# Mixture experts ranked by token count on the chip, with two slot groups for the three emptiest

## The chip, the cores and the metric

The kernel runs on one core of a Trainium2 chip. The metric is device microseconds (us) of one execution; the time given is the median of the timed runs, and one further execution was profiled. The core's engines are named as in the profile: PE (matrix multiply; PEld is its weight load), DVE (vector), ACT (activations), POOL, and SP, which here does little but issue DMAs. [...]

## The reference

A decoder trunk of two layers over 256 tokens of width 1024: retention, a dense SwiGLU, a gated short convolution, and then a mixture of 8 experts, of which each token takes 2. Cut to the mixture, this is what must come out:

```
def _swiglu(xn, w_gate, w_up, w_down):
    return (jax.nn.silu(xn @ w_gate) * (xn @ w_up)) @ w_down

def _moe_swiglu(xn, w_router, w_gate_e, w_up_e, w_down_e):
    logits = (t @ w_router).astype(jnp.float32)      # t: 256 x 1024, 8 experts
    top_vals, top_idx = lax.top_k(logits, TOP_K)     # TOP_K = 2
    gates = ...                                      # softmax over the two
    for e in range(N_EXPERTS):
        h = jax.nn.silu(t @ w_gate_e[e]) * (t @ w_up_e[e])
        out = out + gates[:, e:e + 1] * (h @ w_down_e[e])
```

Each expert has three matrices of 1024 x 3584 float32, 44 MB together. All weights are float32 and are read once. 512 token places (256 tokens, 2 experts each) fall on 8 experts; evaluated with its own inputs, the reference's router gives experts 0 to 7 the counts 60, 62, 69, 73, 65, 53, 76 and 54.

## The kernel before

All weights lie in DRAM as 426 pieces of 1 MiB (128 partitions x 2048 float32): 90 for the dense layers, then 336 for the mixture, 42 for each expert. SP streams them in the order in which they are used (`dma_next`, line 109) into a ring of 14 SBUF tiles called `raw`; three pieces of the mixture's first steps go into spare tiles called `xT` as well. A piece is issued when the tile that it needs has been freed by its last reader, so the ring is at most 14 pieces ahead of PE. SP takes its instructions strictly in order.

The mixture works on gathered tokens. `select` (line 617) marks each token's two experts on DVE, `positions` (line 633) gives each token its slot within its expert, `one_hot` and `gather` (line 673) collect the tokens of an expert into a tile `X` with 96 slots (CAP), three groups of 32. Expert 0 is gathered before the loop, the other seven inside it, in the `hooks` between pieces (`extras`, line 796).

The loop (line 829) has 56 steps, seven for each expert. A step takes four gate and up pieces (`moe_gate_up`) and then the two down pieces of the step before (`moe_down`). The slot groups are the stationary operand, 32 columns at a time, and four matmuls stand beside each other in the four column quarters of the array. So a gate and up piece costs 2 x 3 x 4 matmuls, of which four run at once, and the loop over the groups, `for g in range(NG)` and `for r in range(3)`, sets the count. An expert with 60 tokens takes as long as one with 76.

```
for k in range(2):
    kb = 2 * q + k
    for g in range(NG):
        for j in range(4):
            self.mm(o[g][32 * j:32 * j + 32], X[:, kb, 32 * g:32 * g + 32], w[:, k, j], ...)
```

When an expert is done, `scale_y` (line 717) splits its output on ACT and DVE; one quarter of it lies on partitions 96 to 127 and goes through `yraw` and three small DMAs on ACT's queue into `yq`. `scatter` (line 736) returns the rows to the tokens in two halves, in the next expert's steps 1 and 2. `posrow` and `onehT` hold the positions of one expert, spread over the partitions, for that. The last expert has a form of its own, `last_scatter`. A branch at the end (`fallback`) does the tokens beyond the 96th of any expert; no expert has that many here.

Of the kernel before, what the change touches and what calls it, by code (L numbers as in the profile page):

```python
# [8 lines left out]
F32 = mybir.dt.float32  # L9
# [7 lines left out]
P = 128  # L17
# [11 lines left out]
C_PART = 2640  # L29
C_ALL = 2644  # L30
# [11 lines left out]
NG = CAP // 32  # L42

# [11 lines left out]
class Trunk:  # L55
    def __init__(self, ctx, tc, w, x, gT, gfin, convw, router, cst, eoh, out):
        self.ctx, self.tc, self.nc = ctx, tc, tc.nc
        self.w, self.x, self.convw, self.gfin = w, x, convw, gfin
        self.router, self.cst, self.eoh, self.out, self.gT_dram = router, cst, eoh, out, gT
        self.order = consumption_order()  # L60
        pool = lambda name, bufs, **k: ctx.enter_context(tc.tile_pool(name=name, bufs=bufs, **k))
        self.rawp = pool("raw", R_BUFS)
        self.com = pool("common", 1)
        self.sm = pool("small", 4)
        self.dense = ExitStack()
        pool = lambda name, bufs, **k: self.dense.enter_context(tc.tile_pool(name=name, bufs=bufs, **k))
# [4 lines left out]
        self.raw, self.W = {}, {}  # L71
        self.extra = set()
        self.n_dma = self.n_split = 0
        self.la, self.limit = LA, 2 * N_DENSE - 1
# [524 lines left out]
    def moe(self, base, ev, mp):  # L599
# [8 lines left out]
        lg, sel, off, pos, gts = (small(n, [2, 8]) for n in ("lg", "sel", "off", "pos", "gts"))  # L608
        rs = []
        part = mp.tile([P, 1 + NG], F32, name="part")  # L610
# [6 lines left out]
        def select(tb):  # L617
            nc.vector.tensor_copy(lg[:, tb], pl[tb][:, 0:8])
            le = lg[:, tb, :, None].to_broadcast([P, 8, 8])
            lo = lg[:, tb, None, :].to_broadcast([P, 8, 8])  # L620
            c1 = mp.tile([P, 8, 8], F32, name="c1")
            c2 = mp.tile([P, 8, 8], F32, name="c2")
            rank = mp.tile([P, 8], F32, name="rank")
# [4 lines left out]
            nc.vector.tensor_reduce(rank, c1, axis=AX.X, op=OP.add)  # L628
            nc.vector.tensor_scalar(sel[:, tb], rank, 2.0, None, op0=OP.is_lt)
# [3 lines left out]
        def positions():  # L633
            self.mm(pp[:, 8:16], LT, sel[:, 1], False, True)
            nc.vector.tensor_scalar(off, sel, -1000.0, 1000.0, op0=OP.mult, op1=OP.add)
            nc.vector.tensor_tensor(pos, off, pp[:, 0:16].rearrange("p (a b) -> p a b", a=2), op=OP.add)

        def one_hot(pr, t):
            nc.vector.tensor_tensor(t, iota[:, None, None, :].to_broadcast([P, 2, 2, P]),
                                    pos[:, :, 2 * pr:2 * pr + 2, None].to_broadcast([P, 2, 2, P]), op=OP.is_equal)  # L640
# [14 lines left out]
        def gates2():  # L655
            nc.vector.tensor_tensor(ex, ex, sel, op=OP.mult)
            nc.vector.tensor_reduce(mx, ex, axis=AX.X, op=OP.add)
            nc.vector.reciprocal(mx, mx)
            nc.vector.tensor_tensor(gts, ex, mx[:, :, None].to_broadcast([P, 2, 8]), op=OP.mult)

# [3 lines left out]
        def overflow1():  # L664
            nc.vector.tensor_scalar(fl, pos, CAP - 0.5, None, op0=OP.is_gt)
            nc.vector.tensor_tensor(fl, fl, sel, op=OP.mult)
            nc.vector.tensor_reduce(fr, fl, axis=AX.XY, op=OP.add)
# [26 lines left out]
        def save_positions():  # L694

            self.posT = self.dram.tile([8, S], F32, name="posT")
            for tb in range(2):
                nc.scalar.dma_start(self.posT[:, tb * P:(tb + 1) * P].rearrange("e t -> t e"), pos[:, tb])
# [6 lines left out]
        def slots2(e):  # L705
            row = PT[e]
            if e == NE - 1:
                PT[e] = self.com.tile([P, NG, S], F32R, name="xT", bufs=3)
                for g in range(NG):
                    nc.vector.tensor_scalar(PT[e][:, g], row, part[:, 1 + g:2 + g], None, op0=OP.is_equal)  # L710
            else:
                PT[e] = mp.tile([P, S], F32R, name="onehT")
                nc.vector.tensor_scalar(PT[e], row, part[:, 0:1], None, op0=OP.is_equal)
# [3 lines left out]
        def scale_y(e, accs):  # L717


            yH, yL = (self.xp.tile([P, D], F32R, name=n) for n in ("yH", "yL"))  # L720
            raw = self.xp.tile([P, 768], F32, name="yraw")
# [8 lines left out]
            Y[e] = yH, yL  # L730
# [5 lines left out]
        def scatter(e, hf):  # L736
            f = slice(hf * 512, (hf + 1) * 512)
            ps = [self.ps() for _ in range(2)]
            for tb in range(2):
                for a in range(2):  # L740
                    self.mm(ps[tb], PT[e][0:CAP, tb * P:(tb + 1) * P], Y[e][a][0:CAP, f], a == 0, a == 1)
            for tb in range(2):
                nc.vector.scalar_tensor_tensor(self.h[:, tb, f], ps[tb], gts[:, tb, e:e + 1], self.h[:, tb, f],  # L743
                                               op0=OP.mult, op1=OP.add)

        def last_scatter(accs):
# [3 lines left out]
            for g in (0, 2, 1):  # L750
                self.split(yH[:, g], yL[:, g], accs[g // 2][:, g % 2 * 256:g % 2 * 256 + 256])
            gu = [self.gup.tile([P, 512], F32, name="gu") for _ in range(4)]
            outs = [gu, [self.bank(), self.bank(), self.ps(), self.ps()]]
            for tb in range(2):
                for g in (0, 2, 1):
# [23 lines left out]
        for hf in range(2):  # L779
# [5 lines left out]
                                pos[:, :, 0, None].to_broadcast([P, 2, CAP]), op=OP.is_equal)  # L785
        self.moe_pools()
        for kb in range(0, 8, 2):
            gather(0, (kb, kb + 1), (0,))
        nc.vector.tensor_tensor(t[:, :, 1, 0:CAP], iota[:, None, 0:CAP].to_broadcast([P, 2, CAP]),
                                pos[:, :, 1, None].to_broadcast([P, 2, CAP]), op=OP.is_equal)  # L790
        save_positions()
        nc.scalar.dma_start(part, self.cst[:, C_PART:C_ALL])

        late = {}

        def extras(s):
# [7 lines left out]
            if s == 0:  # L804
                f = {1: gates1}
# [25 lines left out]
        for s in range(MU * NE):  # L831
            e, u = divmod(s, MU)
            hooks = extras(s)
            if s == COUNT_AT:
                n_over = nc.values_load(self.ovf[0:1, 0:1], min_val=0, max_val=NE * S)
            o = self.moe_gate_up(at, XP[e // 2][:, :, e % 2], hooks)
            at += 4
            new = self.moe_swiglu(o)
            if hid is not None:
                if u == 1:  # L840
                    accs = [self.bank(), self.bank()]
                self.moe_down(at, hid, accs, (s - 1) % MU, (s - 1) // MU == NE - 1)
# [3 lines left out]
            hid = self.moe_hid_T(new)  # L846
        gfin = self.com.tile([P, D], F32, name="xT", bufs=3)
        nc.sync.dma_start(gfin, bass.AP(tensor=self.gfin.tensor, offset=self.gfin.offset, ap=[[0, P], [1, D]]))
        self.moe_down(at, hid, accs, MU - 1, True)
# [8 lines left out]
        for hf in range(2):  # L858
            for tb in range(2):
                for q in range(2 * hf, 2 * hf + 2):  # L860
                    hs = self.h[:, tb, q * 256:(q + 1) * 256]
                    nc.vector.scalar_tensor_tensor(hs, outs[tb][q][:, 0:256], gts[:, tb, NE - 1:NE], hs,
# [17 lines left out]
        self.fallback(n_over, mp, pos, gts, tH, tL, iota)  # L880
# [8 lines left out]
    def moe_gate_up(self, at, X, hooks):  # L889


        A, B = (self.gup.tile([P, 512], F32, name="gu") for _ in range(2))
        o = (A[:, 0:256], A[:, 256:512], B[:, 0:256])
        for q in range(4):
            w = self.raw[at + q].rearrange("p (k j c) -> p k j c", k=2, j=4)
            for k in range(2):
                kb = 2 * q + k
                for g in range(NG):
# [4 lines left out]
        return A.rearrange("p (g u c) -> p g u c", g=2, u=2), B[:, 0:256].rearrange("p (g u c) -> p g u c", g=1, u=2)  # L903
# [9 lines left out]
    def moe_hid_T(self, hid):  # L913

        T = self.xp.tile([P, NG, P], F32, name="hT", bufs=2)
        self.nc.vector.transpose(T.rearrange("p g c -> p (g c)"), hid.rearrange("p g c -> p (g c)"))  # L916
        return T

    def moe_down(self, at, T, accs, u, quarters):
# [3 lines left out]
        for d in range(2):  # L923
            w = self.raw[at + d].rearrange("p (k c) -> p k c", k=2)
            for k in range(2):
                j = 2 * d + k
                first, last = u == 0 and j == 0, u == MU - 1 and j == 3
                for r in range(3):
                    o = accs[r // 2][:, r % 2 * 256:r % 2 * 256 + 256]
                    for t in range(4):  # L930
                        g, c = (r, t) if quarters else (t, r) if t < 3 else (r, 3)
# [122 lines left out]
def constants():  # L1054
# [22 lines left out]
    p = np.arange(P)  # L1077
    c[:, C_PART] = p
    for g in range(NG):
# [87 lines left out]
```

## Time and profile before

| | us |
|---|---|
| median of 3 runs | 1483.62 (1483.21 to 1484.95) |
| the profiled execution's own time | 1484.88 |
| its span, first to last instruction | 1483.2 |
| PE busy in the span | 1463.4 (99%) |
| DVE, ACT busy | 461.9 (31%), 304.0 (20%) |

The span has three stretches: the dense layers up to about 540 us, the routing and the first gather up to 558.85 us, and the mixture's loop up to 1467.5 us, after which 15.7 us remain for the last scatter, the final norm and the output. The page's 40 slices are 37 us each. Its DMA row is the mean busy share of the 16 DMA engines in tenths; GB/s is what they moved.

### The profile page before, as it was taken

What the parts mean: (1) busy time and instruction counts of PE and PEld (TensorE: products, weight loads), DVE (VectorE), ACT (ScalarE), POOL (GpSimd) and SP (SyncE); (2) the same over time, 40 slices, a digit from 0 to 9 for tenths busy, and PEclk for the clock granted to TensorE, in tenths of its full rate; (3) what the DMA queues carried; (4) which work ended last, traced back from release to release, by engine and by line L of the source; (5) the groups of instructions that cost most, each with busy time, mean ns of one, the idle gap of its engine ahead of it and who ended that gap; (6) DMA issues with size and microseconds to landing.
All of it is one profiled execution on the core that took longest, in us unless ns stands there. A gap on an engine that the chain in (4) does not pass through costs nothing.

```text
span 1483.2 us, 42711 instructions
## 1 busy us (share of the span) xinstructions
PE 1463.4 (99%) x19924; PEld 1045.7 (71%) x19925; DVE 461.9 (31%) x767; ACT 304.0 (20%) x495; POOL 15.1 (1%) x24
## 2 busy tenths in 40 slices
PE   8999999999999999999999999999999999999996
PEld 7888889999999985665665565666566566566563
DVE  6656566555557651011111101111101211111112
ACT  5444454434435430000000000000000000000001
POOL 0000000000000000000000000000000000000000
PEclk9999999999999989999999999999999999999998
DMA  9944445545454547799999999999999999999980
GB/s 376 380 184 170 157 152 198 209 180 192 171 195 175 199 171 302 308 368 405 371 384 395 389 403 410 370 378 399 383 410 408 378 379 391 382 416 400 386 327 32
DMA packets 69080, 455.31 MB, mean 307 GB/s; under 512 B 10240, under 2 KB 12704, under 8 KB 14752
## 3 DMA queue, kind: packets, MB, share of 16 engines
q1 hardware_dynamic: 62784, 448.82, 77.4%
q10 hardware_dynamic: 6112, 3.69, 1.0%
q8 instruction: 158, 2.59, 0.7%
q14 instruction: 26, 0.21, 0.0%
HBM read 450.73 MB, written 1.06 MB: 305 GB/s over the span
## 4 chain that ended last, share of the span: by engine, by line
PE 97%; DVE 1%; ACT 1%; DMA 0%; issue 0%; POOL 0%; ACTq 0%; POOLq 0%; DVEq 0%
PE gu L143 40%; PE acc L143 30%; PE ps L143 27%; DMA gT<-in_gT 0%; PE ps L367 0%; ACT wh L121 0%; PE ps L229 0%; POOL xT L867 0%; ACT xT L159 0%; ACT junk L210 0%; DVE h L238 0%; DVE xT L161 0%; DVE tL L153 0%; DVE wl L124 0%; DVE vL L153 0%
## 5 line engine op out<-in xcount | busy, mean ns | idle before, releaser
L143 PE MATMUL gu<-raw,X 128*32 128x256 f32 x10704 | 593.9, 380 | 0.0
L143 PEld LDWEIGHTS gu<-raw,X 128*32 128x32 f32 x10704 | 344.5, 110 | 231.6 <-issue 3.9
L143 PE MATMUL acc<-raw,hT 128*32 128x256 f32 x5280 | 295.0, 379 | 0.0
L143 PEld LDWEIGHTS acc<-raw,hT 128*32 128x32 f32 x5280 | 170.6, 110 | 114.9 <-PE ps L143 2.5
L143 PE MATMUL ps<-xT,wh 128*128 128x256 f32 x1536 | 248.2, 280 | 1.0 <-DVE xT L161 1.0
L124 DVE TENSOR_TENSOR wl<-raw,wh 128x1024 fp32r<-128x1024 f32 x180 | 212.6, 1220 | 62.8 <-ACT wh L121 62.6
L143 PEld LDWEIGHTS ps<-xT,wh 128*128 128x128 f32 x1536 | 219.2, 187 | 3.2 <-DVE xT L161 0.7
L121 ACT ACTIVATE wh<-raw 128x1024 fp32r<-128x1024 f32 x180 | 182.2, 1054 | 114.4 <-PE ps L143 91.1
L909 ACT ACTIVATE sg<-gu 128x256 f32<-128x256 f32 x112 | 37.0, 332 | 775.4 <-PE gu L143 773.4
L143 PE MATMUL ps<-xT,wl 128*128 128x256 f32 x768 | 175.7, 279 | 0.0
L910 DVE TENSOR_TENSOR hid<-gu,sg 128x256 f32<-128x256 f32 x112 | 34.7, 352 | 451.3 <-ACT sg L909 451.3
L143 PEld LDWEIGHTS ps<-xT,wl 128*128 128x128 f32 x768 | 127.5, 188 | 0.3 <-DVE wl L124 0.3
L143 PE MATMUL ps<-wh,xT 128*128 128x512 f32 x256 | 72.4, 404 | 2.8 <-ACT wh L121 2.8
L692 DVE TENSOR_SCALAR X<-ps,gT 128x192 f32<-128x192 f32 (+1 forms) x40 | 13.2, 372 | 168.1 <-PE ps L143 168.1
L143 PEld LDWEIGHTS ps<-wh,xT 128*128 128x128 f32 x256 | 47.6, 190 | 14.5 <-ACT wh L121 3.1
L143 PE MATMUL acc<-wh,hH 128*128 128x512 f32 x112 | 43.9, 392 | 0.0
L143 PE MATMUL acc<-wh,hL 128*128 128x512 f32 x112 | 43.7, 390 | 0.0
L743 DVE SCALAR_TENSOR_TENSOR h<-ps,gts,h 128x512 f32<-128x512 f32 x28 | 19.7, 746 | 74.8 <-PE ps L143 74.8
L143 PE MATMUL ps<-wl,xT 128*128 128x512 f32 x128 | 40.7, 399 | 0.0
L143 PE MATMUL acc<-wh,xT 128*128 128x512 f32 x144 | 38.9, 398 | 0.0
L916 DVE STREAM_TRANSPOSE hT<-hid 128x384 f32<-128x384 f32 x56 | 32.3, 577 | 1.7
L143 PEld LDWEIGHTS acc<-wh,xT 128*128 128x128 f32 x144 | 26.7, 188 | 6.0
(168 smaller groups left out, 677.2 us busy)
## 6 DMA issues: line engine op xcount, KB each, us to landing
raw<-in_w SPq DMA_DIRECT2D x420, 1024.0 KB, 7.1
raw<-in_w SPq DMA_DIRECT2D x6, 512.0 KB, 6.4
xT<-in_w SPq DMA_DIRECT2D x3, 1024.0 KB, 4.9
h<-in_x SPq DMA_DIRECT2D x4, 256.0 KB, 4.9
posrow<-posT ACTq DMA_DIRECT2D x8, 128.0 KB, 7.6
mask<-in_cst ACTq DMA_DIRECT2D x4, 192.0 KB, 4.3
yq<-yraw ACTq DMA_DIRECT2D x21, 32.0 KB, 6.9
xT<-in_gfin SPq DMA_DIRECT2D x1, 512.0 KB, 8.1
```

The costliest lines, as they stand in the source:

```text
L121: self.nc.scalar.activation(h, r, AF.Copy)
L124: eng.tensor_tensor(l, r, h.bitcast(F32), op=OP.subtract)
L143: self.nc.tensor.matmul(out, lhsT, rhs, start=start, stop=stop)
L692: nc.vector.tensor_scalar(XP[pr][:, kb, a:b], o, self.gT[:, 3, kb:kb + 1], None, op0=OP.mult)
L743: nc.vector.scalar_tensor_tensor(self.h[:, tb, f], ps[tb], gts[:, tb, e:e + 1], self.h[:, tb, f], op0=OP.mult, op1=OP.add)
L909: nc.scalar.activation(sg[:, f], p[:, :, 0], AF.Silu)
L910: nc.vector.tensor_tensor(hid[:, f], p[:, :, 1], sg[:, f], op=OP.mult)
L916: self.nc.vector.transpose(T.rearrange("p g c -> p (g c)"), hid.rearrange("p g c -> p (g c)"))
```

## The change

The experts run in an order of places. Place 0 is still expert 0; the other seven are ranked on the chip by their token counts, and the places' group counts are fixed: 3, 2, 3, 3, 2, 3, 3, 2. The three emptiest experts of the seven thus run at places 1, 4 and 7 with two groups, 64 slots. The positions and gates are permuted to place order on DVE (`posP`, `gtsP`), and the DMAs of the weights of places 1 to 7 take the expert's number from a register of SP, which is read from the tile `order` in step 2 of the place before. `fallback` takes over when one of these three has more than 64 tokens.

```
+GROUPS = (3, 2, 3, 3, 2, 3, 3, 2)
...
-            self.nc.sync.dma_start(t[:, f], self.w[self.order[j]][:, f])
+        src = self.w[self.order[j]]
+        e, k = divmod(self.order[j] - N_DENSE, 6 * MU)
+        if e > 0:
+            src = self.wm[bass.ds(self.eid[e], 1), k].rearrange("a p c -> p (a c)")
+            self.nc.sync.dma_start(t[:, f], src[:, f])
...
+        nc.scalar.dma_start(part, self.cst[:, C_PART:C_ALL])
...
+            for tb in range(2):
+                self.mm(pp[:, 16:24], ones, sel[:, tb], tb == 0, tb == 1)
+
+        def assign():
+            ranks(rankE, cnt)
+            nc.vector.tensor_tensor(perm, rankE[:, None, :].to_broadcast([P, 8, 8]),
+                                    rank_of[:, :, None].to_broadcast([P, 8, 8]), op=OP.is_equal)
+            nc.vector.tensor_tensor(tmp8, perm, iota[:, None, 0:8].to_broadcast([P, 8, 8]), op=OP.mult)
+            nc.vector.tensor_reduce(ord_, tmp8, axis=AX.X, op=OP.add)
+            nc.vector.tensor_copy(order, ord_)
+            by_place(posP, pos)
+            nc.vector.tensor_scalar(more, rankE, float(sum(g == 3 for g in GROUPS)) - 0.5, 32.0,
+                                    op0=OP.is_gt, op1=OP.mult)
+            nc.vector.tensor_tensor(posF, pos, more[:, None, :].to_broadcast([P, 2, 8]), op=OP.add)
+
+        def by_place(out, src):
+            for tb in range(2):
+                nc.vector.tensor_tensor(tmp8, perm, src[:, tb, None, :].to_broadcast([P, 8, 8]), op=OP.mult)
+                nc.vector.tensor_reduce(out[:, tb], tmp8, axis=AX.X, op=OP.add)
...
         def scale_y(e, accs):
+            if GROUPS[e] == 2:
+                self.split(yH[:, 0:512], yL[:, 0:512], accs[0])
+                return lambda: None
...
+        nc.vector.tensor_tensor(cnt, pp[:, 16:24], big, op=OP.add)
...
-        save_positions()
-        nc.scalar.dma_start(part, self.cst[:, C_PART:C_ALL])
...
             if s == 0:
-                f = {1: gates1}
+                f = {0: assign, 1: second, 2: save_positions, 3: gates1}
...
+            if u == 2 and e + 1 < NE:
+                self.eid[e + 1] = nc.values_load(order[0:1, e + 1:e + 2], engines=[mybir.EngineType.SP],
+                                                 min_val=0, max_val=NE - 1)
...
-                for g in range(NG):
+                for g in range(ng):
...
-                for r in range(3):
+                for r in range(ng):
```

`second` builds the one-hot tile of place 1, which stood ahead of the loop before; `ranks` is the comparison part of the old `select`, made a function. The sums of `sel` over the tokens, two matmuls with `ones`, give the counts; `cnt` puts 512 on top of expert 0's, so that it ranks first. For a place with two groups, `scale_y` needs no `yq`, and `scatter` reads its rows by halves of 64.

PE's own order at place 1, steps 1 and 2 (`gu` and `acc` are the PSUM outputs of gate and up and of down, `hT` the transposed hidden tile, `yH`, `yL` and `onehT` the operands of the scatter). Before:

```order
L143 MATMUL acc<-raw,hT 32x256 x48
L143 MATMUL gu<-raw,X 32x256 x48
L143 MATMUL ps<-yH,onehT 128x512
L143 MATMUL ps<-yL,onehT 128x512
L143 MATMUL gu<-raw,X 32x256 x48
L143 MATMUL acc<-raw,hT 32x256 x48
```

and now:

```order
L149 MATMUL acc<-raw,hT 32x256 x32
L149 MATMUL gu<-raw,X 32x256 x32
L149 MATMUL ps<-yH,onehT 128x512
L149 MATMUL ps<-yL,onehT 128x512
L149 MATMUL gu<-raw,X 32x256 x32
L149 MATMUL acc<-raw,hT 32x256 x32
```

Every run of 48 has become 32; nothing stands elsewhere, and the number of pieces is the same.

SP's order over the mixture. Before:

```order
L109 DMA raw<-in_w 128x2048 x102
L109 DMA xT<-in_w 128x2048 x3
L109 DMA raw<-in_w 128x2048 x55
L835 TENSOR_LOAD ovf
L835 ISA x2
L109 DMA raw<-in_w 128x2048 x263
```

and now, from the same place on:

```order
L115 DMA raw<-in_w 128x2048 x102
L115 DMA xT<-in_w 128x2048 x3
L115 DMA raw<-in_w 128x2048 x10
L881 TENSOR_LOAD order
L881 ISA x2
L115 DMA raw<-in_w 128x2048 x13
L115 ISA
L115 DMA raw<-in_w 128x2048
L115 ISA
```

The register is loaded 13 pieces ahead of its first use, and one more instruction (`ISA`) now stands ahead of the DMA of almost every piece of places 1 to 7.

PE's order between the logits and the first gather (`sel` is the selection, `cm` holds constants, `zero` the warming matmuls). Before, with what each waits for:

```order
L143 MATMUL acc<-sel,cm 128x8 [waits DVE_49]
L190 LDWEIGHTS zero
L190 MATMUL ps<-zero 128x512 [waits PE_49]
L190 LDWEIGHTS zero
L190 MATMUL ps<-zero 128x512
L143 MATMUL ps<-oneh,tH 128x96 [waits DVE_49,PE_49]
```

and now:

```order
L149 MATMUL acc<-sel,cm 128x8 [waits DVE_49] x2
L149 MATMUL acc<-sel,cm 128x8
L196 LDWEIGHTS zero
L196 MATMUL ps<-zero 128x512 [waits PE_49]
L196 LDWEIGHTS zero
L196 MATMUL ps<-zero 128x512
L149 MATMUL ps<-oneh,tH 128x96 [waits DVE_49,PE_49]
```

Two matmuls have come in ahead of the warming ones, and the first of them waits for DVE again. On ACT the DMA of `part` has moved ahead of the two copies that the second half of the logits waits for.

## Rows read from the trace of the kernel before

**Rows 1.** The page: DMA share by slice in tenths, the chain by engine and line

```profile
DMA  9944445545454547799999999999999999999980
...
PE gu L143 40%; PE acc L143 30%; PE ps L143 27%; DMA gT<-in_gT 0%; PE ps L367 0%; ACT wh L121 0%; PE ps L229 0%; POOL xT L867 0%; ACT xT L159 0%; ACT junk L210 0%; DVE h L238 0%; DVE xT L161 0%; DVE tL L153 0%; DVE wl L124 0%; DVE vL L153 0%
```

**Rows 2.** Timeline of the last steps: start, us, engine, line, operation, tiles, count [idle before]

```profile
1431.43 10.54 PE L143 MATMUL gu<-raw,X 128*32 128x256 f32 x192
...
1441.79 5.36 PE L143 MATMUL acc<-raw,hT 128*32 128x256 f32 x96
...
1446.97 10.54 PE L143 MATMUL gu<-raw,X 128*32 128x256 f32 x192
...
1467.51 1.26 ACT L149 ACTIVATE yH<-acc 128x256 fp32r<-128x256 f32 x3 [9.65 <-PE acc L143]
```

**Rows 3.** SP's own waits: who was waited for, us in total, times, longest

```profile
SPq L109 <- PE gu L143: 513.5, 214, 14.5
...
SPq L109 <- PE acc L143: 248.1, 106, 6.8
```

**Rows 4.** Timeline about place 1's first steps: PE's starts, the output's way

```profile
668.88 10.54 PE L143 MATMUL gu<-raw,X 128*32 128x256 f32 x192
...
684.97 2.13 ACTq L726 DMA_DIRECT2D yq<-yraw  x3
...
692.62 0.42 ACT L149 ACTIVATE yH<-yq 96x256 fp32r<-96x256 f32 x1 [4.61 <-DMA yq<-yraw]
```

**Rows 5.** Weight DMAs on SP up to 668.9 us: ns min/median/max, first and last start

```profile
L109 SPq DMA_DIRECT2D raw<-in_w x142: 327/328/448, 1.8 to 666.5; - x142
```

**Rows 6.** DMA view, 668.9 to 1425 us: bytes, queues, issues with us to landing

```profile
DMA packets 42395, 296.61 MB, mean 392 GB/s; under 512 B 4924, under 2 KB 6492, under 8 KB 6492
...
q1 hardware_dynamic: 40265, 293.20, 97.6%
...
raw<-in_w SPq DMA_DIRECT2D x280, 1024.0 KB, 7.4
yq<-yraw ACTq DMA_DIRECT2D x21, 32.0 KB, 6.9
```

**Rows 7.** Stretches: PE, PEld, DVE, ACT, POOL busy, PEclk, DMA share, GB/s

```profile
5.00:10.00 5.00, 2.18 (x11) 1.75 (x10) 2.14 (x5) 3.15 (x6) 0.00 (x0) 0.86 1.00 342
10.00:15.00 5.00, 5.00 (x20) 3.72 (x19) 2.66 (x7) 2.58 (x8) 0.00 (x0) 0.80 1.04 428
...
560.00:565.00 5.00, 5.00 (x84) 2.65 (x80) 0.38 (x3) 0.00 (x0) 2.91 (x1) 0.84 0.19 29
60.00:65.00 5.00, 5.00 (x41) 4.87 (x40) 3.86 (x4) 3.68 (x5) 0.00 (x0) 1.00 1.02 426
10.00:60.00 50.00, 49.93 (x262) 41.66 (x261) 32.80 (x57) 26.92 (x46) 2.23 (x4) 0.98 1.02 419
...
668.90:1425.00 756.10, 756.10 (x13576) 454.43 (x13572) 103.14 (x234) 39.29 (x113) 0.00 (x0) 1.00 1.00 392
```

**Rows 8.** DMA view of the whole span: `part`, KB, us to landing

```profile
part<-in_cst ACTq DMA_DIRECT2D x1, 2.0 KB, 10.0
```

**Rows 9.** Timeline from the second logits to the loop's start

```profile
544.50 3.58 PE L143 MATMUL acc<-gR,xT 128*128 128x8 f32 x16 [0.97 <-ACT xT L587]
...
545.06 0.22 DVE L625 TENSOR_TENSOR c<-lg 128x64 f32<-128x64 f32 x1
...
547.94 1.00 PE L143 MATMUL acc<-sel,cm 128*128 128x8 f32 x4
...
550.17 1.44 PE L190 MATMUL ps<-zero 128*128 128x512 bf16 x3
...
551.17 0.17 DVE L636 TENSOR_TENSOR pos<-off,acc 128x16 f32<-128x16 f32 x1
...
551.88 0.42 PE L143 MATMUL ps<-oneh,tH 128*128 128x96 f32 x1 [0.27 <-DVE oneh L784]
...
570.79 0.62 DVE L910 TENSOR_TENSOR hid<-gu,sg 128x256 f32<-128x256 f32 x2 [10.34 <-ACT sg L909]
```

More of the change, by code (lines that the diff above doesn't have):

```diff
@@ L70, in __init__ @@
         self.psp = pool("ps", 4, space=bass.MemoryType.PSUM)
-        self.raw, self.W = {}, {}
+        self.raw, self.W, self.eid = {}, {}, {}
+        self.wm = w[N_DENSE:NPC].rearrange("(e k) p c -> e k p c", e=NE)
         self.extra = set()
@@ L608, in moe @@
         lg, sel, off, pos, gts = (small(n, [2, 8]) for n in ("lg", "sel", "off", "pos", "gts"))
+        posP, gtsP, posF = (small(n, [2, 8]) for n in ("posP", "gtsP", "posF"))
+        cnt, ord_, rankE, more = (small(n, [8]) for n in ("cnt", "ord", "rankE", "more"))
+        perm, tmp8 = (small(n, [8, 8]) for n in ("perm", "tmp8"))
+        order = mp.tile([P, 8], I32, name="order")
         rs = []
-        part = mp.tile([P, 1 + NG], F32, name="part")
+        part = mp.tile([P, C_ALL - C_PART], F32, name="part")
+        nc.scalar.dma_start(part, self.cst[:, C_PART:C_ALL])
+        rank_of, big = (part[:, c - C_PART:c - C_PART + 8] for c in (C_RANK, C_BIG))
         pl = [self.bank() for _ in range(2)]
@@ L628, in select @@
             nc.vector.tensor_reduce(rank, c1, axis=AX.X, op=OP.add)
+        def select(tb):
+            nc.vector.tensor_copy(lg[:, tb], pl[tb][:, 0:8])
+            rank = mp.tile([P, 8], F32, name="rank")
+            ranks(rank, lg[:, tb])
             nc.vector.tensor_scalar(sel[:, tb], rank, 2.0, None, op0=OP.is_lt)
@@ L708, in slots2 @@
                 PT[e] = self.com.tile([P, NG, S], F32R, name="xT", bufs=3)
-                for g in range(NG):
+                for g in range(GROUPS[e]):
                     nc.vector.tensor_scalar(PT[e][:, g], row, part[:, 1 + g:2 + g], None, op0=OP.is_equal)
@@ L712, in slots2 @@
                 PT[e] = mp.tile([P, S], F32R, name="onehT")
-                nc.vector.tensor_scalar(PT[e], row, part[:, 0:1], None, op0=OP.is_equal)
+                p = part[:, 0:1] if GROUPS[e] == 3 else part[:, 1 + NG:2 + NG]
+                nc.vector.tensor_scalar(PT[e], row, p, None, op0=OP.is_equal)
         Y = {}
@@ L749, in last_scatter @@
             yH, yL = (self.xp.tile([P, NG, 256], F32R, name=n) for n in ("yH", "yL"))
-            for g in (0, 2, 1):
+            gs = (0, 2, 1) if GROUPS[-1] == 3 else (0, 1)
+            for g in gs:
                 self.split(yH[:, g], yL[:, g], accs[g // 2][:, g % 2 * 256:g % 2 * 256 + 256])
@@ L754, in last_scatter @@
             for tb in range(2):
-                for g in (0, 2, 1):
+                for g in gs:
                     for i, y in enumerate((yH, yL)):
@@ L840, in moe @@
                 if u == 1:
-                    accs = [self.bank(), self.bank()]
-                self.moe_down(at, hid, accs, (s - 1) % MU, (s - 1) // MU == NE - 1)
+                    accs = [self.bank() for _ in range(ng - 1)]
+                d = (s - 1) // MU
+                self.moe_down(at, hid, accs, (s - 1) % MU, d == NE - 1, GROUPS[d])
                 at += 2
@@ L879, in moe @@
                 q.dma_start(self.out[tb * P:(tb + 1) * P, cols[hf]], y[:, tb, cols[hf]])
-        self.fallback(n_over, mp, pos, gts, tH, tL, iota)
+        self.fallback(n_over, mp, posF, gts, tH, tL, iota)
     def moe_piece(self, at, hook=None):
@@ L887, in moe_piece, with moe_gate_up @@
             hook()
-    def moe_gate_up(self, at, X, hooks):
-        A, B = (self.gup.tile([P, 512], F32, name="gu") for _ in range(2))
-        o = (A[:, 0:256], A[:, 256:512], B[:, 0:256])
+    def moe_gate_up(self, at, X, hooks, ng):
+        t = [self.gup.tile([P, 512], F32, name="gu") for _ in range(ng - 1)]
+        o = [t[g // 2][:, g % 2 * 256:g % 2 * 256 + 256] for g in range(ng)]
         for q in range(4):
@@ L1077, in constants @@
     p = np.arange(P)
+    c[:, C_RANK:C_RANK + 8] = np.argsort(sorted(range(8), key=lambda i: (-GROUPS[i], i)))
+    c[:, C_BIG] = 2.0 * S
     c[:, C_PART] = p
+    c[:, C_PART + 1 + NG] = p % 64
     for g in range(NG):
```

51 lines of the change are left out of this document (26 added, 25 removed).

## The prediction

> **What bounds the kernel now.** I read four views, from the whole to the part. The page's chain says that the time is PE's: three groups of matmuls hold 97% of it, 40% in gate and up of the mixture and 30% in its down. But the DMA row of the same page is at nines over the whole loop [rows 1], so two engines are at their limits together, and the question is what lies just below PE. The timeline of the last steps gives PE's price: gate and up starts at 1431.43, down at 1441.79, the next gate and up at 1446.97, so a step costs 10.36 + 5.18 = 15.54 us, for 6 pieces: 2.59 us a piece [rows 2]. Then SP's own waits: it waited 513.5 us for gate and up and 248.1 us for down, 2.4 us at a time, nearly the pace of a piece [rows 3]. It waits for PE to free a tile and for little else: the ring is full, the transfers follow PE. Last the DMA views: in the loop the core moves 392 GB/s, which is PE's demand, gathers and scatters included [rows 6, 7]. While the first ring was being filled, with PE no limit to it, it moved 419 GB/s over 50 us, and 426 in a late 5 us of that [rows 7]. The reader is to see that the DMAs have 7% in hand over PE and no more.
>
> **The change, part by part.** *Two groups.* A step of a two-group expert keeps 128 of 192 matmul instructions: 10.36 instead of 15.54 us [rows 2]. Over 21 steps PE is relieved of 21 x 5.18 = 108.8 us. If PE stayed the bound all through, the span would be 1483.2 - 108.8 = 1374.4 us.
>
> *But no piece goes.* A two-group piece takes PE 10.36 / 6 = 1.73 us, that is 607 GB/s, which no row shows. So I count in transfers, from the start of place 1, at 668.88 us [rows 4]. Up to there SP has issued 142 DMAs of `raw`, the last at 666.5 [rows 5]; two pieces took two each, and three went to `xT`, so that is 143 of 426 pieces, and 283 are left. What is a piece's price when the queue is never empty? A piece is 1.0486 MB; all bytes over weight bytes in the loop are 296.61 / 293.20 = 1.012 [rows 6], a little less with the `yq` transfers of three experts gone: 1.010. At 419 GB/s that is 2.53 us a piece. At 426 it is 2.49, at the loop's 392 it is 2.70; these are the ends. I take 2.53, since the 50 us at 419 are the one long stretch in which the DMAs, not PE, set the pace, and that is the state in question.
>
> *Is the queue never empty?* Place 1 begins with about 11 pieces landed ahead (14 less 7.4 us of landing at 2.7 us each [rows 6]). PE wants 42 pieces in 42 x 1.73 = 73 us, some 80 with gathers and scatter; the DMAs bring 80 / 2.53 = 32. 11 + 32 is just 42: place 1 hardly waits, but leaves the ring drained. Places 2 and 3 use 84 pieces in about 225 us, in which 89 come: the ring gets back 5. Place 4 wants 42 in 76 us, has 5 + 30, and must wait 7 x 2.53 = 17 us. Places 5 and 6 give back 5 again, place 7 waits another 17. From place 1 on the ring is never full for long, so the DMAs run without a pause, and the end is theirs.
>
> *The routing ahead of the loop.* Two count matmuls come in, and the first waits for DVE, since it writes the bank that `pos` reads: `pos` ends at 551.34. Two such matmuls took 1.00 us (four instructions), and the three warming ones behind them 1.44 us; so PE reaches the gather at about 551.5 + 1.0 + 1.4 = 553.9 instead of 551.88: +2.0 [rows 9]. The `part` DMA now stands on ACT ahead of the copies that PE waits for (0.97 us idle at 544.50 [rows 9]); an issue on this queue costs 2.13 / 3 = 0.7 us [rows 4], so +0.6. It lands 10.0 us later [rows 8], at about 554, and `cnt` on DVE waits for it with the gather's evacuations behind; PE has two PSUM tiles to fill meanwhile, 3.4 us of matmuls, so I cost this wait at 0, and at 2 us without that cover. In all **+2.6** (0 to 5). The ranking itself is 15 DVE operations of about 0.22 us, 3.3 us, in a step in which DVE idles 10.34 us until the first `hid` [rows 9]: 0. The same holds for the four operations that permute the gates.
>
> *SP.* An issue takes 0.33 us [rows 5]; the register form adds one sequencer instruction to it, and no row shows its price. From below it is nothing; from above, SP has 2.4 us of waiting per piece to spend [rows 3]. I take 0, nearest to the one issue that is seen. The load of the register stands 13 pieces ahead of its use, so that even 10 us there would be hidden by the pieces in flight.
>
> *The output's way.* `yq` needs 2.1 + 6.9 us [rows 4, 6], and its split on ACT came 7.7 us after the first issue (684.97 to 692.62). In a two-group place the second half of the scatter comes after 5 + 2 pieces and more, 13 us: still in time, and where it isn't, in a stretch that waits for transfers anyway: 0. At place 7 the last scatter has two groups instead of three; of the 15.7 us behind the last matmul about 1.0 goes.
>
> *The sum.* The last piece issued before place 1 lands at 666.5 + 7.4 = 673.9; + 2.6 for the later start; + 283 x 2.53 = 716.0; the last landing is at 1392.5. Behind it PE has half a piece, 0.9, and the end, 14.7: a span of **1408**, 75 us less than 1483.2. The median of the runs is 0.4 above the profiled span (1483.62), the profiled execution itself 1.7; I say **1408** for the median. With 2.49 us a piece it is 1397, with 2.70 it is 1456.
>
> **The rivals.** *A. The loop's rate is its ceiling.* The DMA share is 1.00 at 392 GB/s as it is 1.02 at 419 [rows 7]; read by the share, the engines are as busy and nothing is in hand. Against it: PE sets the pace there, and a share that is 1.00 at 392 and 1.02 at 426 doesn't tell the two apart. At 2.58 to 2.70 us a piece: 1422 to 1456. [...]
>
> *B. The DMAs are quicker than I think.* At 426 GB/s or above [rows 7] and a start without the 2.6 us: 1376 to 1396, the lower end being PE's own floor of 1374.4 with the routing and the end counted in.
>
> [...]
>
> *D. The other side: register-addressed issues bind SP.* The place is SP's queue in places 1 to 7, 280-odd issues, in order. It decides from (1483.2 - 15.6 - 676.5) / 283 = 2.80 us a piece: an issue of 3.0 us, nine times the 0.33 seen, gives 676.5 + 849 + 15.6 = 1541. Nothing in the profile speaks for so much; but no register-addressed issue ran.
>
> *E. The change doesn't do what it says:* one of the three emptiest has over 64 tokens and the fallback reads all experts again. With 53, 54 and 62 tokens it doesn't; its two passes over 336 pieces would cost 672 x 2.53 = 1700 us.
>
> **How the numbers follow.** My forecast, DMA-bound at about 2.49 to 2.57 us a piece, 1396 to 1422: 0.65. A 0.16, B 0.09, C 0.05, D 0.03, E and others 0.02. The range 1388 to 1436 takes in half of B and half of A. Faster by more than 0.2% (3 us, about what a measurement here can tell from no change) is everything but D, E and a rest: 0.95; same 0.01; slower 0.04.
>
> **What would show it.** Right: the DMA slices at 415 to 423 GB/s from about 675 us to the end; PE without waits in place 1, with idle time put down to the `raw` DMAs in places 4 and 7, some 15 to 20 us each; landings of 10 us and more instead of 7.4; PE within a piece or two of the last landing at the end; the loop's first matmul 2 to 3 us later. Wrong: DMA share 1.00 with 390 to 400 GB/s while PE waits (A); PEclk under 0.9 over whole places (C); gaps in the DMAs with SP waiting for nothing (D).

## The result and the profile after

The changed kernel takes 1430.92 us (median of 4 runs, 1429.11 to 1432.39), the kernel before 1484.17 beside it (1483.21 to 1484.95): ratio 0.9641, 95% interval 0.9624 to 0.9658. That is 53 us less, inside the range of 1388 to 1436, 23 us above the 1408 forecast and above the 1396 to 1422 that had been given 0.65. The profiled execution has a span of 1427.5 us, 19.5 above the sum.

The page of the changed kernel: PEclk, the granted TensorE clock as a share of full speed, DMA share (both in tenths) and GB/s in 40 slices, then the chain by engine and by group.

```profile
PEclk9999999999999997999999999999999999999998
DMA  9954544544555544989999999999999999999896
GB/s 375 389 182 149 192 167 185 199 177 177 181 201 179 189 172 118 368 304 377 408 419 419 419 419 406 392 420 419 387 421 420 418 420 419 396 421 418 347 422 252
PE 44%; DMA 16%; issue 1%; DVE 0%; POOL 0%; ACT 0%; SPq 0%; ACTq 0%; POOLq 0%; DVEq 0%
PE gu L149 28%; DMA raw<-in_w 14%; PE acc L149 14%; PE ps L149 2%; DMA posrow<-posT 1%; DMA yq<-yraw 0%; POOL xT L918 0%; DVE tL L159 0%; SPq L115 0%; PE ps L196 0%; DVE h L913 0%; DVE yL L156 0%; DVE xT L926 0%; ACTq L770 0%; ACT yH L155 0%
```

Beside [rows 1] two things are new. The chain, which was 97% PE, now has the weight DMAs in it (the page gives no engine for the rest of the chain), and most slices of the loop stand at 418 to 422 GB/s, with dips to 406, 392, 387, 396 and 347. Where PE waits shows in its own waits from place 1 on (us in total, times, longest), and in places 4 and 7 alone, asked for each by its stretch:

```profile
PE gu L149 <- DMA raw<-in_w: 21.9, 35, 1.7
PE acc L149 <- DMA raw<-in_w: 11.2, 20, 0.9
...
PE gu L149 <- DMA raw<-in_w: 10.5, 17, 1.0
PE acc L149 <- DMA raw<-in_w: 5.3, 9, 0.9
...
PE gu L149 <- DMA raw<-in_w: 10.1, 16, 1.7
PE acc L149 <- DMA raw<-in_w: 5.9, 11, 0.7
```

Place 4 waits 15.8 us and place 7 16.0; the first place with two groups, place 1, waits 1.3 us. The stretches that answer to [rows 7] (PE, PEld, DVE, ACT, POOL busy, PEclk, DMA share, GB/s): nearly the whole of places 1 to 7, a gap, and PE's waiting stretches of places 4 and 7.

```profile
685.00:1380.00 695.00, 668.43 (x11776) 398.37 (x11772) 94.34 (x211) 32.63 (x91) 0.00 (x0) 1.00 1.00 411
890.00:895.00 5.00, 5.00 (x100) 3.01 (x95) 0.30 (x1) 0.00 (x0) 0.00 (x0) 1.00 0.64 227
1025.00:1050.00 25.00, 18.68 (x312) 9.33 (x304) 1.98 (x5) 0.77 (x2) 0.00 (x0) 1.00 1.01 423
1375.00:1400.00 25.00, 19.63 (x332) 10.17 (x328) 0.98 (x3) 0.38 (x1) 0.00 (x0) 1.00 1.01 420
```

The granted clock, for which this trace has two levels, 1.00 and 0.50, stays at 1.00 while PE is busy for 18.68 us of 25. The transfers run at 420 to 423 GB/s there, but at 411 over the whole. SP's waits say what interrupts them; they answer to [rows 3]:

```profile
SPq L115 <- DMA raw<-in_w: 456.4, 219, 9.7
...
SPq L115 <- PE gu L149: 105.9, 52, 17.2
SPq L115 <- DMA posrow<-posT: 57.1, 7, 13.2
SPq L115 <- PE acc L149: 40.9, 21, 5.9
SPq L115 <- DMA yq<-yraw: 38.6, 8, 12.3
```

SP waited for PE and now waits for DMAs, and not for weight DMAs alone: 95.7 us went on two kinds of small transfers that ScalarE issues. The trace has eight DMA semaphores, which SP's and ScalarE's transfers both use, 50 to 55 weight DMAs on each; a weight DMA waits until the transfer that had its semaphore last has landed: on the six semaphores whose landings the trace has in full, all 316 weight DMAs that follow another transfer start after its landing, the median 0.12 us after. ScalarE issues its transfers at PE's pace (the `posrow` transfer at 1342.46 us stands behind an activation that waited 12.30 us for PE), and SP, none of whose 1492 instructions overlap in the trace, stands still until one has been issued and landed: 5.6 us for that one.

Last the start of the loop, where [rows 9] end: PE's timeline of the changed kernel, the first selection matmul and step 0.

```profile
545.35 0.73 PE L149 MATMUL acc<-sel,cm 128*128 128x8 f32 x4
...
558.01 10.29 PE L149 MATMUL gu<-raw,X 128*32 128x256 f32 x139
568.99 0.41 PE L149 MATMUL gu<-raw,X 128*32 128x256 f32 x2 [0.69 <-issue]
571.50 5.05 PE L149 MATMUL gu<-raw,X 128*32 128x256 f32 x88 [2.10 <-issue]
578.61 1.99 PE L149 MATMUL gu<-raw,X 128*32 128x256 f32 x25 [2.06 <-issue]
```

The loop begins no later than before, but PE stands still three times in the first step, and the row gives no releaser. The 142nd weight DMA, at 666.5 in [rows 5], now comes at 674.6.

### The profile page after: what moved, and what is told of

Read it like the earlier page. It is cut to its first block, busy times and chain, and to the rows that moved or that the text cites. A ratio compares the mean times of both kernels' runs of the same rounds, so it can differ in the third digit from the quotient of the medians.

```text
span 1427.5 us, 39207 instructions
## 1 busy us (share of the span) xinstructions
PE 1368.6 (96%) x17896; PEld 987.4 (69%) x17897; DVE 454.5 (32%) x756; ACT 296.2 (21%) x469; POOL 15.2 (1%) x24
## 3 DMA queue, kind: packets, MB, share of 16 engines
HBM read 450.74 MB, written 1.06 MB: 317 GB/s over the span
## 4 chain that ended last, share of the span: by engine, by line
PE 44%; DMA 16%; issue 1%; DVE 0%; POOL 0%; ACT 0%; SPq 0%; ACTq 0%; POOLq 0%; DVEq 0%
PE gu L149 28%; DMA raw<-in_w 14%; PE acc L149 14%; PE ps L149 2%; DMA posrow<-posT 1%; DMA yq<-yraw 0%; POOL xT L918 0%; DVE tL L159 0%; SPq L115 0%; PE ps L196 0%; DVE h L913 0%; DVE yL L156 0%; DVE xT L926 0%; ACTq L770 0%; ACT yH L155 0%
## 5 line engine op out<-in xcount | busy, mean ns | idle before, releaser
L149 PE MATMUL gu<-raw,X 128*32 128x256 f32 x9360 | 531.1, 382 | 26.7 <-DMA raw<-in_w 21.9
L149 PEld LDWEIGHTS gu<-raw,X 128*32 128x32 f32 x9360 | 309.2, 110 | 232.6 <-DMA raw<-in_w 30.2
L149 PE MATMUL acc<-raw,hT 128*32 128x256 f32 x4608 | 262.1, 380 | 11.3 <-DMA raw<-in_w 11.2
L149 PEld LDWEIGHTS acc<-raw,hT 128*32 128x32 f32 x4608 | 150.0, 110 | 115.5 <-issue 11.6
L960 ACT ACTIVATE sg<-gu 128x256 f32<-128x256 f32 (+1 forms) x91 | 31.1, 342 | 748.0 <-PE gu L149 746.5
L961 DVE TENSOR_TENSOR hid<-gu,sg 128x256 f32<-128x256 f32 (+1 forms) x91 | 30.6, 368 | 435.4 <-ACT sg L960 435.4
L787 DVE SCALAR_TENSOR_TENSOR h<-ps,gtsP,h 128x512 f32<-128x512 f32 x28 | 19.7, 745 | 72.9 <-PE ps L149 72.9
L149 PE MATMUL acc<-wl,hH 128*128 128x512 f32 x112 | 30.9, 389 | 0.0
```

Of the source, the lines that this page charges most:

```text
L149: self.nc.tensor.matmul(out, lhsT, rhs, start=start, stop=stop)
L960: nc.scalar.activation(sg[:, f], p[:, :, 0], AF.Silu)
L961: nc.vector.tensor_tensor(hid[:, f], p[:, :, 1], sg[:, f], op=OP.mult)
```

## The experiments

Two things were to be told apart: what the start costs, and what the transfers lose between 419 and 411 GB/s. One table first, each run against the kernel before on the same chip. The 142nd issue is the last start in the row of SP's first 142 `raw` DMAs.

| run | median us | ratio (95%) | 142nd issue |
|---|---|---|---|
| changed kernel | 1430.92 | 0.9641 (0.9624 to 0.9658) | 674.6 |
| e1 small DMAs on GpSimd | 1428.37 | 0.9614 (0.9598 to 0.9630) | 678.4 |
| e2 position rows on GpSimd | 1430.41 | 0.9639 (0.9623 to 0.9655) | 675.2 |
| e3 ranking, three groups | 1495.38 | 1.0072 (1.0055 to 1.0089) | 677.6 |
| e4 half of each piece | 1383.67 | 0.9321 (0.9306 to 0.9337) | 674.3 |
| e5 before, write moved in the code | 1484.83 | 1.0000 (0.9990 to 1.0009) | 668.4 |
| e6 positions as rows | 1422.97 | 0.9588 (0.9572 to 0.9604) | 667.5 |
| e7 order fixed in the code | 1431.68 | 0.9638 (0.9622 to 0.9654) | 678.3 |
| e8 e6 and e1 together | 1418.98 | 0.9556 (0.9540 to 0.9572) | 668.4 |
| e9 before, write delayed | 1491.10 | 1.0043 (1.0030 to 1.0055) | 674.1 |
| e10 e3 with positions as rows | 1486.94 | 1.0016 (1.0006 to 1.0026) | 670.0 |
| e11 e8 with one late gap | 1422.87 | 0.9591 (0.9578 to 0.9604) | 668.8 |

**e4: are transfers the bound?** From the 18th piece of the mixture on, each transfer brings the first half of its piece alone, and the matmuls use that half twice; PE's matmuls stay, and the issues but for one (425 instead of 426).

```diff
+        if j >= N_DENSE + 17:
+            cuts = [slice(0, 1024)]
...
-                        self.mm(o[g][32 * j:32 * j + 32], X[:, kb, 32 * g:32 * g + 32], w[:, k, j],
+                        self.mm(o[g][32 * j:32 * j + 32], X[:, kb, 32 * g:32 * g + 32], w[:, 0, j],
```

> Changed kernel that transfers only the first half of every mixture piece from the eighteenth on and uses that half twice, so its output is not the reference's; PE's instructions are the same in number and shape. It takes away the transfers as a bound. If the transfers are all that stands between PE's relief and the time: PE's floor, 1484 - 108.8 + 5 to 8 for the start - 1 for the end = 1379 to 1383. Rival P (PE loses time in two-group places by itself, to the shorter steps, the output's way or the clock): 1390 or more, with PE idle on ACT or DVE.

1383.67 us, and no wait of PE for a weight is left in the loop. The span is 1382.4, near the sum of PE's floor in the prediction, 1374.4, and the 7.8 us by which the 142nd issue is late. The 47 us from there to 1430.9 are transfers.

**e1 and e2: the semaphores in rotation.** The small transfers are issued by GpSimd and go on a queue of their own (q0 in e1's DMA view, 816 packets from 690 to 1400 us); e2 moves the first of the two lines alone.

```diff
-            nc.scalar.dma_start(PT[e], self.posT[e:e + 1, :].broadcast_to([P, S]))
+            nc.gpsimd.dma_start(PT[e], self.posT[e:e + 1, :].broadcast_to([P, S]))
...
-                nc.scalar.dma_start(q[32 * i:32 * i + 32], raw[CAP:P, 256 * i:256 * i + 256])
+                nc.gpsimd.dma_start(q[32 * i:32 * i + 32], raw[CAP:P, 256 * i:256 * i + 256])
```

> Changed kernel, with the small DMAs of the output's way (posrow, yq) issued from POOL instead of ACT; nothing is left out. Theory S (shared semaphores): the weight DMAs on SP wait for the landing of the eighth DMA before them in the program, ACT's small ones included; ACT issues these only at PE's pace, so SP stands still (57 us on posrow, 39 us on yq in the changed kernel's trace) and the DMA engines run dry for some 14 us in all. With the small DMAs on another queue, SP's waits on posrow and yq are gone, the DMA rate from 700 us on is 418 to 420 GB/s without dips, and the time is 1431 - 14 = 1417 (1412 to 1421). Rival R (register-addressed issue, or the weight stream itself, limits the rate): no difference, 1429 to 1433.

> Changed kernel, with only the posrow DMAs issued from POOL; nothing is left out. Theory S: SP's waits on posrow go, those on yq stay; the deepest dips of the DMA rate (227 GB/s at 890 us, 334 over 1325 to 1350 us) stand behind yq, so less than half of the gain: 1426 (1422 to 1429). Rival R: 1429 to 1433.

In e1 SP waits for no small transfer any more, after 95.7 us in the changed kernel, and from 685 to 1380 us the core moves 417 GB/s instead of 411; the time falls by 2.5 us where about 14 had been expected (the intervals of the two ratios still overlap), and e2 gains nothing that can be told. So SP's standing still is real, and almost free. The reason comes with e8 and e11.

**e3, e7: the ranking and the register.** e3 ranks and addresses by register, but keeps three groups everywhere; e7 keeps the ranking and has the same order of experts written in the code.

```diff
-GROUPS = (3, 2, 3, 3, 2, 3, 3, 2)
+GROUPS = (3, 3, 3, 3, 3, 3, 3, 3)
```

```diff
-            src = self.wm[bass.ds(self.eid[e], 1), k].rearrange("a p c -> p (a c)")
+            src = self.w[N_DENSE + 6 * MU * (0, 1, 6, 3, 7, 2, 4, 5)[e] + k]
...
-                self.eid[e + 1] = nc.values_load(order[0:1, e + 1:e + 2], engines=[mybir.EngineType.SP],
-                                                 min_val=0, max_val=NE - 1)
```

> Changed kernel with three groups at all places: ranking, permuted gates and register-addressed weights alone, against the kernel before; nothing is left out. PE is the bound as before. Theory S with the start as measured: the routing ahead of the loop and the stalls in the loop's first step cost 5 to 8 us, the register form nothing: 1489 to 1492, with no wait of PE for weight DMAs after the first step. Rival R (register form costs SP or the rate): above 1495, with PE waiting for weights. If it is 1484 to 1486, the start costs nothing and the stalls seen there were of that one execution.

> The changed kernel, with the ranking still made on the chip, but the weight transfers addressed by constants (the same order of experts written in the code), no register loaded and none in an address. Theory (the register form costs nothing in the issue, since SP waits for landings anyway): 1428 to 1433 us, ratio 0.962 to 0.966, and a piece takes 2.56 to 2.58 us as in the changed kernel. Rival (the register form of the issue lengthens each piece, 2.53 forecast against 2.57 measured): a piece at 2.53 us, 283 x 0.04 = 11 us less, 1418 to 1421 us.

Constant addresses change nothing (1431.68 us, inside the changed kernel's range), and from its 142nd issue on e3 keeps the kernel before's pace: 284 issues from 677.6 to 1443.3, 2.70 us each, as from 666.5 to 1432.1. PE waits for no weight in e3's loop. So no price of the register form shows, although e3's time is just above the 1495 that was to speak for one: e3 is 11.3 us slower, more than the 5 to 8 expected, but its 142nd issue is 11.1 us late, so all of it is lost before place 1.

**e5, e6, e9, e10: the write of the positions.** What else had moved? The table of positions goes to memory in two DMAs of 4-byte elements. Before, they were issued at 551.4 and 551.8 us and landed 10.4 us later, while next to no weights moved (0 to 4 GB/s from 553 to 563 us); now they wait for the ranking, are issued at 561 and fly during step 0, when weights are wanted. e6 turns the table with two transposes on TensorE and writes 8 rows in one DMA; e10 does the same with three groups everywhere. e5 and e9 try the reverse on the kernel before, which has no ranking: e5 moves the call to step 0's third piece, e9 puts idle ScalarE copies ahead of it.

```diff
+            p = self.ps()
             for tb in range(2):
-                nc.scalar.dma_start(self.posT[:, tb * P:(tb + 1) * P].rearrange("e t -> t e"), posP[:, tb])
+                nc.tensor.transpose(p[0:8, tb * P:(tb + 1) * P], posP[:, tb], self.ident)
+            row = mp.tile([P, S], F32, name="posTs")
+            nc.vector.tensor_copy(row[0:8], p[0:8, 0:S])
+            nc.scalar.dma_start(self.posT, row[0:8])
```

```diff
-        save_positions()
...
-                f = {1: gates1}
+                f = {1: gates1, 2: save_positions}
```

```diff
             self.posT = self.dram.tile([8, S], F32, name="posT")
+            for _ in range(18):
+                nc.scalar.activation(self.junk, self.zero, AF.Copy)
```

> The kernel before, with one edit: the positions' table is written to memory (two DMAs of 4-byte elements, 10 us each to land) from the hook of step 0's third piece, where the changed kernel writes it, instead of just ahead of the loop. Theory T (this scattered write, issued while the loop starts, holds up what TensorE needs in steps 0 to 1): the first silu of the loop comes some 4 to 6 us later than before's 570.4, TensorE has waits put down to 'issue' in steps 0 and 1, and all weights after them are late by as much: 1488 to 1494 us, ratio 1.003 to 1.007. Rival (the late start of the changed kernel comes from its count and ranking on VectorE and the select step): 1483 to 1485 us, first silu within 1 us of before's.

> The changed kernel, with the positions' table turned by two transposes on TensorE (PSUM, one copy on VectorE) and written as 8 rows of 1 KB in one DMA, in place of two DMAs of 4-byte elements. Theory T: the issue waits of steps 0 and 1 go, the first silu comes at most 13 us after the loop's start (16.3 in the changed kernel, 11.6 before), and the time falls by 4 to 8 us to 1423 to 1427 us. Rival (the ranking's own work delays the start): 1429 to 1433 us, ratio as the changed kernel's 0.964.

> The kernel before, with 18 idle ScalarE copies (zeros to an unused tile, 0.5 to 0.55 us each) ahead of the two scattered position writes, so that these are issued near 561 us, inside step 0, as in the changed kernel, and not at 551.4. Nothing else is added and the ranking isn't there. Theory T (the scattered write holds up what TensorE needs while it flies): TensorE has 'issue' waits of 3 to 6 us in steps 0 and 1, the first silu comes 3 to 5 us later than before's, the time is 1488 to 1493 us, ratio 1.003 to 1.006. Rival (the ranking is needed too, the place of the write alone does nothing): no issue waits, 1483 to 1486 us.

> Ranking and register addresses, three slot groups everywhere, and the positions written as 8 rows in one DMA. By theory T the 11.3 us that the ranking cost with the scattered write shrink to the count products and their wait, 1 to 3 us: 1485 to 1487 us, ratio 1.001 to 1.002. Rival (the write is a small part, VectorE's ranking chain and the register addresses are the rest): 1490 to 1494 us.

e6 gains 8 us, and e10 takes 1486.94 us, inside its 1485 to 1487. e5 is no test: ScalarE had nothing ahead of the call, and issued the write at 551.9 as ever. e9 is the test, and 6.7 us slower than the kernel before, with nothing of the ranking in it (the small DMA of `part` comes later with the write there). Its ScalarE and PE timelines:

```profile
549.24 11.85 ACT L698 ACTIVATE junk<-zero 128x512 bf16<-128x512 bf16 x18
560.52 1.03 ACTq L700 DMA_DIRECT2D posT<-pos  x2
...
568.69 0.93 PE L143 MATMUL gu<-raw,X 128*32 128x256 f32 x6 [0.80 <-issue]
570.13 5.86 PE L143 MATMUL gu<-raw,X 128*32 128x256 f32 x101 [0.51 <-issue]
578.58 1.82 PE L143 MATMUL gu<-raw,X 128*32 128x256 f32 x24 [2.60 <-issue]
```

The stalls without a releaser are there again, within 1.5 us of the same times. What is missing then shows in the DMA view of 561 to 575.5 us (queue, kind: packets, MB, share of 16 engines; issues with us to landing). The kernel before:

```profile
q1 hardware_dynamic: 586, 4.29, 77.5%
q8 instruction: 2, 0.03, 0.8%
...
raw<-in_w SPq DMA_DIRECT2D x5, 1024.0 KB, 6.3
```

The changed kernel:

```profile
q1 hardware_dynamic: 106, 0.87, 45.8%
q10 hardware_dynamic: 2080, 0.01, 6.5%
...
raw<-in_w SPq DMA_DIRECT2D x4, 1024.0 KB, 12.4
```

2080 packets carry 0.01 MB, the weights move 0.87 MB instead of 4.29, and the two packets of instructions are not there at all; e9 has 1.06 MB and none either. PE stands still because its instructions come late: that is a reading of the absent row together with waits that name no releaser, not a direct record. The next packet of instructions bears it out. It starts at 576.3 us in the changed kernel, where the DMA view of 576 to 577 us has its row, at 576.2 in e9 and at 579.4 in e3, and PE's last stall ends 2.3 to 2.4 us later in each (578.61, 578.58 and 581.66); in the other four runs with this write in step 0 it is 2.2 to 4.4 us.

```profile
q8 instruction: 1, 0.02, 6.0%
```

The stalls are 4.9 us in the changed kernel. More goes in what follows them: the granted clock, 1.00 from 565 to 575 us, falls: it is 0.50 in each half microsecond from 580 to 583 us and 1.00 from 583.5, a mean of 0.68 from 580 to 585 us, and 68 matmuls begin there, where e6, without the stalls, has 1.00 and 100. First the changed kernel, then e6:

```profile
580.00:585.00 5.00, 5.00 (x68) 3.32 (x64) 0.00 (x0) 0.00 (x0) 0.00 (x0) 0.68 1.00 418
...
580.00:585.00 5.00, 5.00 (x100) 3.02 (x96) 1.60 (x6) 0.66 (x2) 0.00 (x0) 1.00 1.01 390
```

In e6, with 8 rows, both are back (2 instruction packets, 4.01 MB), and PE streams:

```profile
558.45 10.17 PE L149 MATMUL gu<-raw,X 128*32 128x256 f32 x144
568.55 0.38 PE L737 MATMUL ps<-ident,posP 128*8 128x128 f32 x2
568.86 13.16 PE L149 MATMUL gu<-raw,X 128*32 128x256 f32 x240
```

The table sorts the same way: the 142nd issue comes at 674 to 678 wherever the scattered write flies in step 0, and at 666.5 to 670 wherever it doesn't, whatever else the kernel has.

**e8 and e11: why are SP's pauses almost free?** e8 joins the edits of e6 and e1; e11 gives one late pause back, those two transfers of the last places.

```diff
-            nc.gpsimd.dma_start(PT[e], self.posT[e:e + 1, :].broadcast_to([P, S]))
+            (nc.scalar if e == 7 else nc.gpsimd).dma_start(PT[e], self.posT[e:e + 1, :].broadcast_to([P, S]))
...
-                nc.gpsimd.dma_start(q[32 * i:32 * i + 32], raw[CAP:P, 256 * i:256 * i + 256])
+                (nc.scalar if e == 6 else nc.gpsimd).dma_start(q[32 * i:32 * i + 32], raw[CAP:P, 256 * i:256 * i + 256])
```

> Both edits together: the positions written as 8 rows, and the expert loop's small transfers (position rows, rescaled rows of the second down half) issued by GpSimd instead of ScalarE, so that they no longer take turns with the weight transfers. If the two effects add (2.5 us measured for the second alone, 4 to 8 expected of the first): 1420 to 1425 us, ratio 0.957 to 0.960. If the scattered write costs nothing: 1427 to 1430 us.

> As the run before with the rows and the small transfers on GpSimd (1419.0 us), but the second down half's rescaled rows of place 6 and the position row of place 7 go back to ScalarE's queue, so that SP's weight DMAs stand still once, near 1316 us: 12 us and then 6 us of waiting for them, with a stretch of 5 us at 110 GB/s and two more under 380, which taken alone is 5.2 us of transfers lost (3.7 + 0.5 + 1.0 at 419 GB/s). Theory H: through 700 us of uninterrupted streaming half of the sixteen DMA engines fall behind the other half, by up to 15 us, and the end waits for the slow half (208 GB/s at a DMA share of 0.50 in the last 15 us); a pause in issuing lets them catch up and costs nothing: 1418 to 1420 us, and the half-rate tail at the end is gone or shorter than 8 us. Rival (all sixteen engines are alike, every gap is lost time): 1423 to 1425 us, and the tail of half rate stays.

e8 is the fastest version, 1418.98 us, 4.0 under e6. Its stretches: the loop, then the end (columns as above).

```profile
685.00:1380.00 695.00, 669.11 (x11784) 399.22 (x11780) 93.22 (x210) 32.19 (x90) 10.10 (x20) 1.00 1.01 416
...
1385.00:1390.00 5.00, 3.71 (x68) 1.82 (x63) 0.00 (x0) 0.00 (x0) 0.00 (x0) 1.00 0.89 357
1390.00:1395.00 5.00, 3.85 (x70) 1.98 (x64) 0.87 (x2) 0.38 (x1) 0.00 (x0) 1.00 0.51 208
1395.00:1400.00 5.00, 3.94 (x74) 2.10 (x66) 0.00 (x0) 0.00 (x0) 0.00 (x0) 1.00 0.50 207
```

With the last pieces still in flight the rate halves and the share, a mean over the sixteen engines, halves with it. The packets of the trace say how: from 1370 to 1380 us there are never fewer than sixteen in flight, from 1390 to 1400 always eight to ten and mostly eight, and a packet of 8 KB takes 0.31 us in both. Read by that, half of the engines have nothing left while the other half works on as fast as before. e1, whose SP has no pauses either, ends in the same way:

```profile
1400.00:1405.00 5.00, 3.87 (x72) 2.01 (x64) 0.87 (x2) 0.38 (x1) 0.00 (x0) 1.00 0.50 205
1405.00:1410.00 5.00, 3.93 (x72) 2.09 (x65) 0.00 (x0) 0.00 (x0) 0.00 (x0) 1.00 0.51 211
```

Up to 1380 the core had been ahead at 416 GB/s, e6 at 410; e8 pays this back at the end. In e11 the end is another one:

```profile
1300.00:1325.00 25.00, 25.00 (x452) 14.85 (x448) 4.56 (x10) 1.94 (x5) 0.00 (x0) 1.00 0.77 296
...
1390.00:1395.00 5.00, 3.90 (x68) 1.90 (x72) 0.00 (x0) 0.00 (x0) 0.00 (x0) 1.00 1.01 423
1395.00:1400.00 5.00, 3.92 (x68) 2.11 (x72) 0.87 (x2) 0.38 (x1) 0.00 (x0) 1.00 1.01 418
1400.00:1405.00 5.00, 4.34 (x80) 2.67 (x80) 0.00 (x0) 0.00 (x0) 0.00 (x0) 1.00 0.91 365
```

The tail at half rate is gone, as theory H had it; but the time is 1422.87, not 1418 to 1420, and just under the rival's 1423 to 1425. Neither held whole. The pause left out 25 x (419 - 296) / 419 = 7.3 us of transfers and cost 3.9 us: so about half of it came back in the tail, by this reckoning. And this one pause costs as much as all of e6's (1422.97): the earlier pauses cost nothing that can be told. Their rows fit, 227 GB/s at a share of 0.64 in the changed kernel at 890 us, near the half rate, with never fewer than eight packets in flight, as if mostly the engines that are ahead rested there; the late pause, with two small transfers one after the other, goes deeper (110 GB/s at 0.32 in the changed kernel from 1325 to 1330).

## Why the prediction was right, and what was off

**The bound.** As forecast, the transfers took over from PE: 283 pieces from place 1 on, 418 to 423 GB/s where nothing interrupts them, 15.8 and 16.0 us of waiting in places 4 and 7 (17 each forecast), 1.3 in place 1 ("hardly"), a landing time of 19.7 us instead of 7.4 [rows 6], and PE two pieces from its end at the last wait (1408.60, 3.66 us of matmuls). e4 shows it from the other side. The mechanism was right, then; the number owes something to the width of the range. Two terms were too small and both missed the same way, and 1430.9 lies in the range only because that took in half of rival A's.

**The terms.** The sum had 666.5 + 7.4 + 2.6 + 716.0 + 15.6 = 1408; the span is 1427.5.

- *The start, 2.6 forecast, 8.1 measured* (674.6 - 666.5): +5.5. The routing ahead of the loop, which is what the 2.6 stood for, was costed a little high: from the first selection matmul to the loop PE takes 10.9 us before (547.94 [rows 9] to 558.85) and 12.7 in the changed kernel (545.35 to 558.01), +1.8 where the sum had +2.0; of the +0.6 on ScalarE nothing shows, PE idles 1.0 us for those copies in both. That the loop's first matmul is not 2 to 3 us later, as the prediction's sign had it, but 0.8 earlier, is because this execution reached the selection 2.6 us sooner. e10, which has the ranking without the scattered write, is 2.6 us slower in its time. What failed is a step that the prediction did not cost at all: the change moves the positions' write from ahead of the loop into step 0, and with it two DMAs of 2048 elements. It alone costs 6.7 us in the kernel before (e9) and 8.0 in the changed one (e6).
- *The price of a piece, 2.53 forecast, 2.58 measured:* 1.0486 MB x 1.010 at 411 GB/s, x 283 = 729.3 instead of 716.0: +13.3. By the reading above, the 419 GB/s of [rows 7] is the rate of a stretch in which the engines that are ahead run further ahead, and the price of a landed piece over 700 us is that of the slower half. Without any pause it is still 2.56: in e8 the last weight DMA is issued at 1383.9 and lands 17.6 us later, (1401.5 - 668.4 - 7.4) / 283. The pauses are the rest, 4 us of time by e8 against e6.
- *The end, 14.7 behind the last matmul on weights forecast, 15.2 measured* (1408.60 + 3.66 to 1427.5): +0.5.

5.5 + 13.3 + 0.5 = 19.3, and the distance between the sum and the span is 19.5.

**The register and SP's issue** were rightly taken at nothing (e7). **The rivals.** A's mechanism falls: 420 GB/s runs where the loop before had 392, and PE waits there; but the lower end of its price, 2.58 us a piece, is what the whole loop came to. B falls by the same rows; neither stretch of 25 us is above 423. C, a granted clock that falls where PE waits, fails for places 4 and 7, with 1.00 through both waiting stretches; where the clock did cost time is step 0, behind the stalls, and there the prediction had not looked for it. D falls by e7, E by the time itself.

**What stays open.** Why one half of the DMA engines, by the reading above, falls behind. The instruction packets are a candidate: in the changed kernel's DMA view of 682 to 1410 us there are 95 of 16 KB with a share of 0.9%, 0.009 x 728 x 16 = 105 us of one engine's time. If they fell on half of the engines, that would be 13 us for each of these, near the length of e8's tail. The trace doesn't tell the engines apart, so this is an estimate and was not tried. One indication is there: the only packet of instructions within each tail (e8 at 1392.9 us, e1 at 1402.6) is one of the eight in flight and not a ninth, so it fell to the half that was still working. Two packets are no proof.

## What to carry to other kernels

When a change makes the producer of a small table later, look where its write will fly then: 2048 elements of 4 bytes left no stall where next to no weights moved, and cost 7 to 8 us at the start of a loop that needs weights and instructions at the same time; two transposes and 8 rows took the stall away. When a kernel turns from compute-bound to transfer-bound, price a transfer by the interval between landings over a long stretch (2.58 us here), not by the GB/s of a short one (2.53), and look at the DMA share in its last 15 us: 0.50 at 207 GB/s, after 1.01 at 416, was read here as engines that were not level.

## What the runs showed that was not expected

- ScalarE's DMA queue, at PE's pace, stopped SP's: SP waited 95.7 us for small transfers that ScalarE had issued or was still to issue, on the eight semaphores that both use; on GpSimd's queue that wait was gone (e1). The pauses cost 2.5 to 4.0 us in all (e1, at the edge of what can be told; e8 against e6).
- While the scattered 4-byte writes flew, weight pieces landed after 12.4 us instead of 6.3, and no instruction packet moved in the 14.5 us looked at.
- With PE 75% and 79% busy in the two stretches shown, and 53 waits of 0.6 us on average in places 4 and 7, the granted clock stayed at 1.00 there; behind the stalls of step 0, of 0.7, 2.1 and 2.1 us, it fell, to a mean of 0.68 over 5 us.
